# Queries and keys of attention: float16 parts split as rows and turned by DMA transposes, in place of identity products on TensorE

## The chip, the core and the metric

The program runs on one core of one Trainium2 chip. The core has these engines, each with its own queue of instructions that it works through in order: TensorE (PE, with its weight loads shown apart as PEld), VectorE (DVE), ScalarE (ACT), GpSimd (POOL) and SyncE (SP), which in this kernel issues nearly all DMAs. Sixteen DMA engines move the data. The metric is the device time of one execution in microseconds (us). One execution was also taken by the hardware profiler; its instructions, waits and transfers are the views that are shown here.

## The reference, cut to what matters

One layer of a transformer over 2048 rows (latents) and 256 rows (context) of width 1024: a modulated norm, one input projection, a retention branch and an attention branch, an output projection, and a feed-forward part. The change is in what attention does with its queries and keys, so only that is shown:

```python
q = _apply_rope(_rmsnorm(aq.reshape(B, L, ATT_HEADS, ATT_HD), q_norm_g), *att_cs)
k = _apply_rope(_rmsnorm(ak.reshape(B, L, ATT_KV_HEADS, ATT_HD), k_norm_g), *att_cs)
v = av.reshape(B, L, ATT_KV_HEADS, ATT_HD)
kc = _rmsnorm(cak.reshape(B, Lc, ATT_KV_HEADS, ATT_HD), k_norm_g)
...
k_all = jnp.concatenate([k_ctx, k_lat], axis=1)
...
s = jnp.einsum('bqkgd,bskd->bkgqs', q, k).astype(jnp.float32) * ATT_SCALE
p = jax.nn.softmax(s, axis=-1).astype(v.dtype)
return jnp.einsum('bkgqs,bskd->bqkgd', p, v)
```

There are 8 query heads and 2 key/value heads of width 64; four query heads share one key head. All inputs are float32.

## The kernel before, in words

*Accuracy by parts.* TensorE is given float16. A float32 operand is split into a high part, its rounding to float16, and a low part, the rest, also in float16. A score q.k is then q_hi k_hi + q_hi k_lo + q_lo k_hi. With a head width of 64 only half of TensorE's 128 rows are needed for one such product, so two of them are stacked in one matmul of 128 rows.

*First stage (0 to about 600 us).* The input projection. The rows come in 18 tiles of 128 (2 of context, 16 of latents) and in two groups: the first six tiles (context and latents 0 to 3), then latents 4 to 15. For each group and each block of columns of the weight (`C_RQ`, `C_RK`, `C_RV`, `C_RG` for retention, `C_AQ` for attention's queries, `C_AKV` for its keys and values) there is one *unit* per tile: 24 matmuls (8 blocks of depth, three products of parts) into one bank `pso`, of which there are five. The order of units is written out in `PLAN`: in the first group all `AKV` units follow each other, then all `AQ` units; in the second group `RK` and `AKV` alternate, then `AQ` and `RQ` alternate (from tile 15 down), then `RG`.

What happens to a unit's result is planned by hand. `post` hands pieces of work to `do(step, part, function)`: step s + 2 means "after the matmuls of the second unit from here". `run_step` emits a step's parts in the order of `PARTS`: hi, evac, turned, low, vec, pool, root, aux, turn, load, store. Since every engine works in order, this list is also the order of each queue. The steps carry much else: the weights' own splits, loads of later weights, the largest magnitudes of the feed-forward weights (`greatest_of`: a load one step, a DVE reduction `wmx` from `wm` the next), the forward states of retention.

*Queries (unit s of `AQ`).* ACT copies the bank to `xs` (L698), squares it (L658); DVE and POOL make norm and rotation (`rope`), the result is `ys` (L647, L649), 128 rows by 512 in float32. Step s + 4: four products with the identity turn it into `psx` in PSUM (L710, `turn`), so that rows become columns; partition 64 e + d then holds element d of head 2 j + e. Step s + 5: ACT makes the high part from `psx` (L781), DVE the low part (L784), both into `qhl`, a tile with tag `zs` (two buffers, shared with the turned retention queries and keys, L739). Step s + 6: the tile is stored to `aq` in DRAM (L788).

*Keys (unit s of `AKV`).* After norm and rotation `kn` holds keys as rows. Step s + 4: ACT makes the high part `kh` (L828). Step s + 5: DVE subtracts (L831), and `kn` holds key and low part beside each other. Step s + 6: two products with the identity (L836), one for each key head, give 128 partitions: 64 of the key and 64 of its low part. Step s + 7: DVE copies both into `ks` as float16 (L841), the tile from which all scores are made, 128 partitions by 2 heads by 2304 keys. At the end of the stage (L1521, L1522) `ks2` is made by DMA: the high parts again, in its lower 64 partitions, and a constant table `unit` in its upper 64.

*Second stage (about 600 to 1480 us).* Attention runs in 32 groups (16 query tiles, two key heads), 18 steps each, beside retention, the output projection and the start of the feed-forward part. `Group.load` fetches a group's queries `qr` 14 steps before its first use, with four DMAs of 64 KB: high parts in `qr[:, 0]`, low parts in `qr[:, 1]`, each in the lower and again in the upper 64 partitions. A first pass (`piece`, L177 and L181; `maximum`, L190) finds each query's largest score, with one matmul per 512 keys: `qr[:, 0]` against `ks`. Its shift is written as two float16 parts into the upper partitions of `qr[:, 1]` (`turn`, L204). The second pass (`scores`, L210 and L211) adds two matmuls, `ks` with `qr[:, 0]` and `ks2` with `qr[:, 1]`; `exp` follows, then the split of the weights and the product with the values. The first group's loads and first pass already run in the last units of the first stage.

*Third stage.* The feed-forward part, not touched.

Of the kernel before, what the change touches and what calls it, by code (L numbers as in the profile page):

```python
# [22 lines left out]
P = 128  # L23
# [9 lines left out]
HD = 64  # L33
# [23 lines left out]
def layer_kernel(ctx: ExitStack, tc: tile.TileContext, a: dict, out: bass.AP):  # L57
# [34 lines left out]
    aq_d = scratch("aq", NT, [P, 2, 4, P], F16)  # L92
# [56 lines left out]
    class Group:  # L149
# [7 lines left out]
        def load(self):  # L157
            pool, tag = (mq, "mb") if self.n % 4 < 2 else (qp, "qr")
            self.qr = pool.tile([P, 2, 4, P], F16, name="qr", tag=tag, bufs=2)
            q = self.qr.rearrange("p x (j e) t -> p x j e t", e=2)  # L160
            for e in range(2):
                src = aq_d[self.t][64 * e : 64 * e + 64, :, 2 * self.g : 2 * self.g + 2]
                nc.sync.dma_start(q[:64, :, :, e], src)
                nc.sync.dma_start(q[64:, :, :, e], src)
# [105 lines left out]
    with ExitStack() as st, tc.manual_schedule():  # L270
# [417 lines left out]
        def post(s, g, col, kind, i, x):  # L688
# [73 lines left out]
            elif col == C_AQ:  # L762
# [14 lines left out]
                do(s + 4, "turn", turn)  # L777

                def high():
                    x["z"] = op.tile([P, 2, 4, P], F16, name="qhl", tag="zs")  # L780
                    nc.scalar.activation(x["z"][:, 0], x["pt"], AF.Copy)  # L781

                def low():
                    nc.vector.tensor_tensor(x["z"][:, 1], x["pt"], x["z"][:, 0], op=ALU.subtract)  # L784

                do(s + 5, "turned", high)
                do(s + 5, "vec", low)
                do(s + 6, "store", lambda: nc.sync.dma_start(aq_d[i], x["z"]))  # L788
            else:
# [5 lines left out]
                def new_k():  # L795
                    x["kn"] = op.tile([P, 2, 2, HD], F32, name="kn", tag="kn", bufs=4)
                    return x["kn"][:, :, 0]

                r = lambda: bc(x["r"].unsqueeze(2), [P, 2, HD])
                if kind == "c":  # L800

                    def plain():
# [7 lines left out]
                        lambda: nc.vector.tensor_tensor(x["kn"][:, :, 0], x["kn"][:, :, 0], r(), op=ALU.mult),  # L810
# [15 lines left out]
                def high():  # L826
                    x["kh"] = op.tile([P, 2, HD], F16, name="kh", tag="kh")
                    nc.scalar.activation(x["kh"], x["kn"][:, :, 0], AF.Copy)  # L828

                def low():  # L830
                    nc.vector.tensor_tensor(x["kn"][:, :, 1], x["kn"][:, :, 0], x["kh"], op=ALU.subtract)  # L831

                def turn_k():
                    x["pt"] = psT.tile([P, 4, P], F32, name="psx", tag="psx")
                    for g in range(2):
                        nc.tensor.transpose(x["pt"][:, g], x["kn"][:, g].rearrange("p a b -> p (a b)"), ident)  # L836
# [3 lines left out]
                do(s + 6, "turn", turn_k)  # L840
# [1636 lines left out]
```

## Time and profile before

| | |
|---|---|
| median of 3 runs | 2655.08 us (2653.93 to 2656.46) |
| profiled execution, its own time | 2656.33 us |
| its span on the core | 2654.5 us |
| granted TensorE clock | 0.998 |
| first `L710` for queries to last query store | 122.5 to 564.2 us |
| DMA issued by SP, whole span | 478.94 MB, 54.8% of 16 engines |

The profile names lines of the kernel file (L710) and tiles by their names in the program. A row of a group has, in this order: engine, operation, output and inputs, shapes, count, busy time, mean duration of one, idle time of the engine just before and what ended it. A row of waits reads: engine and instruction, what it waited for, total us, times, longest. A row of one tile's instructions gives smallest, median and largest duration in ns, and the first and last start. "SPq" is a DMA issue on SyncE's queue; its duration is the time for which the issue holds that queue, and the time to landing is counted from the issue until the data have arrived. Matmuls overlap: a row of 0.38 us can start 0.22 us after the one before it.

### The profile page before, as it was taken

To read this page: it belongs to the slowest core of one execution; us is meant where nothing else is said; L and a number is where in the kernel's file an instruction comes from. 1 tells how busy PE (TensorE), PEld (TensorE's weight loads), DVE (VectorE), ACT (ScalarE), POOL (GpSimd) and SP (SyncE) were. 2 spreads that over 40 slices of the span, in tenths; PEclk is the share of its full clock that TensorE was granted. 3 is DMA by queue.
4 is the path that set the end of the run, shared out by engine and by line. 5 is a ranking of instruction groups with operands and counts; after the bars stand their busy time and mean duration, and the time that the engine had idled before them with its cause. 6 is when DMAs were issued, how large, how long until landed. Compare 5 with 4: busy or idle time off the path is not lost.

```text
span 2654.5 us, 45435 instructions
## 1 busy us (share of the span) xinstructions
PE 2601.0 (98%) x16617; PEld 1450.9 (55%) x16617; DVE 2049.4 (77%) x3099; ACT 1504.7 (57%) x2544; POOL 1761.7 (66%) x1451
## 2 busy tenths in 40 slices
PE   8999999998999999999999999999999999999998
PEld 5875555545666666666666444444444444444443
DVE  5778798677888888988987597889876656655686
ACT  3856343425877778788878575666665322222243
POOL 3644566545676668888887696677662666666686
PEclk9999999999999999999999999999999999999999
DMA  7876899746022123333422754776685757475453
GB/s 231 272 252 207 303 330 323 257 119 218 25 84 72 57 65 116 96 84 92 128 77 80 259 170 150 230 241 231 208 297 144 278 180 287 165 293 174 160 187 114
DMA packets 332903, 481.84 MB, mean 182 GB/s; under 512 B 90228, under 2 KB 200068, under 8 KB 328200
## 3 DMA queue, kind: packets, MB, share of 16 engines
q1 hardware_dynamic: 332664, 478.94, 54.8%
q8 instruction: 130, 2.13, 0.3%
q14 instruction: 93, 0.76, 0.1%
q10 hardware_dynamic: 16, 0.01, 0.0%
HBM read 321.89 MB, written 156.38 MB: 180 GB/s over the span
## 4 chain that ended last, share of the span: by engine, by line
PE 69%; ACT 3%; POOL 2%; DVE 1%; DMA 1%; issue 0%; SPq 0%; POOLq 0%; DVEq 0%; ACTq 0%
PE pd L2290 7%; PE pd L2289 7%; PE pd L2288 7%; PE pu L2063 7%; PE pu L2061 7%; PE pu L2062 7%; PE st L210 4%; PE o L245 4%; PE st L211 4%; PE mp L177 3%; PE o L243 2%; PE bank L1832 2%; PE bank L1830 2%; PE bank L1831 2%; ACT p L216 1%; ACT phi L220 1%
## 5 line engine op out<-in xcount | busy, mean ns | idle before, releaser
L190 DVE TENSOR_REDUCE nm<-mp 128x1 f32<-128x512 f32 x558 | 377.6, 685 | 90.7 <-PE mp L177 85.4
L216 ACT ACTIVATE p<-st 128x512 f32<-128x512 f32 x576 | 341.4, 600 | 162.7 <-PE st L211 156.3
L227 POOL TENSOR_TENSOR plo<-p,phi 128x1024 f16<-128x1024 f32 x160 | 348.2, 2181 | 87.1 <-ACT phi L220 87.0
L2063 PE MATMUL pu<-hf,w1f 128*128 128x512 f16 x896 | 339.6, 379 | 0.0
L2290 PE MATMUL pd<-w,uf 128*128 128x512 f16 x896 | 339.6, 379 | 0.0
L2061 PE MATMUL pu<-hf,w1f 128*128 128x512 f16 x896 | 339.6, 379 | 0.0
L2289 PE MATMUL pd<-w,uf 128*128 128x512 f16 x896 | 339.6, 379 | 0.0
L2062 PE MATMUL pu<-hf,w1f 128*128 128x512 f16 x896 | 339.6, 379 | 0.0
L2288 PE MATMUL pd<-w,uf 128*128 128x512 f16 x896 | 339.6, 379 | 0.0
L2308 POOL TENSOR_TENSOR y<-y,d 128x512 f32<-128x512 f32 x128 | 210.4, 1646 | 146.6 <-ACT uf L2277 99.9
L220 ACT ACTIVATE phi<-p 128x1024 f16<-128x1024 f32 x288 | 305.2, 1060 | 0.0
L229 DVE TENSOR_TENSOR plo<-p,phi 128x512 f16<-128x512 f32 x256 | 240.1, 939 | 21.8 <-ACT phi L220 9.4
L243 PE MATMUL o<-wv,plo 128*128 128x65 f16 x2304 | 230.7, 193 | 0.3 <-POOL plo L227 0.2
L245 PE MATMUL o<-wv,phi 128*128 128x129 f16 x2176 | 229.0, 220 | 0.0
L210 PE MATMUL st<-qr,ks 128*128 128x512 f16 x576 | 218.3, 379 | 8.6 <-ACT p L216 6.3
L243 PEld LDWEIGHTS <-plo 128*128 128x128 f16 x2304 | 205.5, 98 | 30.4 <-POOL plo L227 2.4
L2300 DVE SCALAR_TENSOR_TENSOR y<-pd,scy,y 128x512 f32<-128x512 f32 x160 | 116.9, 747 | 132.3 <-PE pd L2290 132.1
L211 PE MATMUL st<-qr,ks 128*128 128x512 f16 x576 | 218.5, 379 | 0.0
L2073 DVE TENSOR_TENSOR r<-pu,r 128x512 f32<-128x512 f32 x224 | 150.0, 684 | 82.8 <-PE pu L2063 58.3
L1191 PE MATMUL pso<-wf,h_l 128*128 128x512 f16 (+1 forms) x576 | 208.2, 361 | 0.0
L1192 PE MATMUL pso<-wf,h_l 128*128 128x512 f16 (+1 forms) x576 | 208.1, 361 | 0.0
L1193 PE MATMUL pso<-wf,h_l 128*128 128x512 f16 (+1 forms) x576 | 208.1, 361 | 0.0
(389 smaller groups left out, 6116.2 us busy)
## 6 DMA issues: line engine op xcount, KB each, us to landing
wm<-in_w_ff SPq DMA_DIRECT2D x64, 512.0 KB, 7.1
u<-r SPq DMA_DIRECT2D x128, 256.0 KB, 4.4
ur<-u SPq DMA_DIRECT2D x128, 256.0 KB, 5.9
y<-x SPq DMA_DIRECT2D x64, 512.0 KB, 6.5
wf<-w2f SPq DMA_DIRECT2D x112, 256.0 KB, 2.9
w<-wf SPq DMA_DIRECT2D x28, 1024.0 KB, 10.0
w1r<-in_w_ff SPq DMA_DIRECT2D x48, 512.0 KB, 5.3
x<-y SPq DMA_DIRECT2D x48, 512.0 KB, 2.6
```

What stands on the lines that cost most here:

```text
L190: nc.vector.tensor_reduce(dst, src, axis=AX.X, op=ALU.max, negate=True)
L216: nc.scalar.activation(self.p[kt // 2][:, kt % 2], self.s.pop(kt), AF.Exp, scale=HD**-0.5)
L220: nc.scalar.activation(hi, self.p[j], AF.Copy)
L227: nc.gpsimd.tensor_tensor(lo, p, hi, op=ALU.subtract)
L243: mm(o[:, : HD + 1], lo[:, i, c], v[:, : HD + 1], start=False, stop=False)
L245: mm(o, hi[:, i, c], v[:, :VW], start=False, stop=last)
L2061: mm(pu[hf, i], whi, hi, start=k == 0, stop=False)
L2062: mm(pu[hf, i], whi, lo, start=False, stop=False)
L2063: mm(pu[hf, i], wlo, hi, start=False, stop=k == 3)
L2288: mm(ps, u[:, 0, b], w[:, b, 0], start=b == 0, stop=False)
L2289: mm(ps, u[:, 0, b], w[:, b, 1], start=False, stop=False)
L2290: mm(ps, u[:, 1, b], w[:, b, 0], start=False, stop=b == 3)
```

## The change

The split is made before the turn. Queries stay rows: the tile `z` holds, for each head, 64 high and then 64 low parts, and it is stored so. Loading a group turns it: a DMA with `transpose=True` takes 128 rows by 512 columns (four heads of 128) and lays each head's 128 columns on 128 partitions. Each of the two halves of `qr` is loaded this way from the same rows, so both now hold high parts in the lower and low parts in the upper 64 partitions. For keys, ACT writes the high part twice side by side (`kk`), and a DMA transpose lays it straight into `ks`, high parts in both halves; the low parts (`kl`) are turned by a second DMA into `kt`, which is stored to DRAM two steps later; `ks2` reads its lower half from there. So `qr[:, 0]` with `ks` now gives q_hi k_hi + q_lo k_hi, and `qr[:, 1]` with `ks2` gives q_hi k_lo and the shift; before, the first gave q_hi k_hi + q_hi k_lo. The largest scores of the first pass are taken over the new sum.

```diff
-    aq_d = scratch("aq", NT, [P, 2, 4, P], F16)
+    aq_d = scratch("aq", NT, [P, 2, 4 * P], F16)
+    kl_d = dram.tile([P, NK, P], F16, name="kl", tag="kl")
...
         def load(self):
             pool, tag = (mq, "mb") if self.n % 4 < 2 else (qp, "qr")
             self.qr = pool.tile([P, 2, 4, P], F16, name="qr", tag=tag, bufs=2)
-            q = self.qr.rearrange("p x (j e) t -> p x j e t", e=2)
-            for e in range(2):
-                src = aq_d[self.t][64 * e : 64 * e + 64, :, 2 * self.g : 2 * self.g + 2]
-                nc.sync.dma_start(q[:64, :, :, e], src)
-                nc.sync.dma_start(q[64:, :, :, e], src)
+            for x in range(2):
+                nc.sync.dma_start(self.qr[:, x], aq_d[self.t][:, self.g], transpose=True)
...
-                do(s + 4, "turn", turn)
 
                 def high():
-                    x["z"] = op.tile([P, 2, 4, P], F16, name="qhl", tag="zs")
-                    nc.scalar.activation(x["z"][:, 0], x["pt"], AF.Copy)
+                    x["z"] = op.tile([P, 8, 2, HD], F16, name="qhl", tag="zs")
+                    nc.scalar.activation(x["z"][:, :, 0], heads(x["y"], 8), AF.Copy)
 
                 def low():
-                    nc.vector.tensor_tensor(x["z"][:, 1], x["pt"], x["z"][:, 0], op=ALU.subtract)
-
-                do(s + 5, "turned", high)
+                    nc.vector.tensor_tensor(x["z"][:, :, 1], heads(x["y"], 8), x["z"][:, :, 0], op=ALU.subtract)
+
+                def store():
+                    nc.sync.dma_start(aq_d[i].rearrange("p g n -> p (g n)"), x["z"].rearrange("p h a d -> p (h a d)"))
+
+                do(s + 4, "turned", high)
                 do(s + 5, "vec", low)
-                do(s + 6, "store", lambda: nc.sync.dma_start(aq_d[i], x["z"]))
+                do(s + 5, "store", store)
...
                 def high():
-                    x["kh"] = op.tile([P, 2, HD], F16, name="kh", tag="kh")
-                    nc.scalar.activation(x["kh"], x["kn"][:, :, 0], AF.Copy)
+                    x["kk"] = op.tile([P, 2, 2, HD], F16, name="kk", tag="kk")
+                    x["kl"] = op.tile([P, 2, HD], F16, name="kl", tag="kl")
+                    for e in range(2):
+                        nc.scalar.activation(x["kk"][:, :, e], x["kn"], AF.Copy)
 
                 def low():
-                    nc.vector.tensor_tensor(x["kn"][:, :, 1], x["kn"][:, :, 0], x["kh"], op=ALU.subtract)
+                    nc.vector.tensor_tensor(x["kl"], x["kn"], x["kk"][:, :, 0], op=ALU.subtract)
 
                 def turn_k():
-                    x["pt"] = psT.tile([P, 4, P], F32, name="psx", tag="psx")
-                    for g in range(2):
-                        nc.tensor.transpose(x["pt"][:, g], x["kn"][:, g].rearrange("p a b -> p (a b)"), ident)
+                    x["kt"] = op.tile([P, 1, P], F16, name="kt", tag="kt")
+                    to = ks[:, :, row * P : (row + 1) * P]
+                    nc.sync.dma_start(to, x["kk"].rearrange("p g e d -> p (g e d)"), transpose=True)
+                    nc.sync.dma_start(x["kt"], x["kl"].rearrange("p g d -> p (g d)"), transpose=True)
 
                 do(s + 4, "hi", high)
                 do(s + 5, "low", low)
-                do(s + 6, "turn", turn_k)
-                do(s + 7, "vec", lambda: nc.vector.tensor_copy(ks[:, :, row * P : (row + 1) * P], x["pt"][:, :2]))
+                do(s + 5, "store", turn_k)
+                do(s + 7, "store", lambda: nc.sync.dma_start(kl_d[:, row], x["kt"][:, 0]))
...
     ks2 = vp.tile([P, 2, NK * P], F16, name="ks2")
     for g in range(2):
-        nc.sync.dma_start(ks2[:64, g], ks[:64, g])
+        nc.sync.dma_start(ks2[:64, g], kl_d[64 * g : 64 * g + 64].rearrange("d n t -> d (n t)"))
         nc.sync.dma_start(ks2[64:, g], a["unit"])
```

The tiles `kk`, `kl` and `kt` come from the pool `op`, which gives two buffers to each tag.

More of the change, by code (lines that the diff above doesn't have):

```diff
@@ L795, in new_k @@
                 def new_k():
-                    x["kn"] = op.tile([P, 2, 2, HD], F32, name="kn", tag="kn", bufs=4)
-                    return x["kn"][:, :, 0]
+                    x["kn"] = op.tile([P, 2, HD], F32, name="kn", tag="kn", bufs=4)
+                    return x["kn"]
                 r = lambda: bc(x["r"].unsqueeze(2), [P, 2, HD])
```

2 lines of the change are left out of this document (1 added, 1 removed).

## The prediction

> **What bounds the kernel now.** I read the page first, then the busy time by stretches, then who waited for whom, then single instructions.
>
> ```profile
> span 2654.5 us, 45435 instructions
> PE 2601.0 (98%) x16617; PEld 1450.9 (55%) x16617; DVE 2049.4 (77%) x3099; ACT 1504.7 (57%) x2544; POOL 1761.7 (66%) x1451
> ...
> 300.00:425.00 125.00, 122.56 (x713) 70.26 (x712) 113.78 (x160) 53.65 (x97) 84.79 (x97) 1.00 0.95 339
> 425.00:600.00 175.00, 170.30 (x871) 87.84 (x869) 119.23 (x224) 56.22 (x91) 90.45 (x95) 1.00 0.64 207
> ...
> 660.00:2654.00 1994.00, 1973.34 (x13104) 1061.51 (x13101) 1552.33 (x2249) 1196.05 (x2005) 1414.62 (x1061) 1.00 0.48 158
> ```
>
> The columns of the stretches are window, length, busy time of PE, PEld, DVE, ACT and POOL, granted clock, DMA share, GB/s. PE is busy 98% of the span and of both stretches in which keys and queries are made (300 to 425 and 425 to 600 us); DMA is at 0.95 in the first. All of the edit's arithmetic lies before 660 us; the rest only follows. So the question is whether PE really sets the pace there. PE's waits between 0 and 660 us, longest first (total, times, longest):
>
> ```profile
> PE mp L177 <- DVE wmx L190: 3.6, 3, 2.1
> PE mp L177 <- ACT xs L698: 3.3, 2, 2.3
> PE mp L181 <- DVE wmx L190: 3.1, 1, 3.1
> ```
>
> The longest is 3.6 us: PE waits for almost nothing, so work taken from its queue there should shorten the stage, as long as no other queue takes over.
>
> **What is removed.** Four identity products per query tile (64 of the 192 of L710) and two per key tile (L836). Their durations overlap, so I take the price from start to start:
>
> ```profile
> 443.92 0.38 PE L1193 MATMUL pso<-wf,h_l 128*128 128x512 f16 x1
> 444.14 0.60 PE L710 MATMUL psx<-ident,ys 128*128 128x128 f32 x4
> 444.58 0.38 PE L1191 MATMUL pso<-wf,h_l 128*128 128x512 f16 x1
> ...
> 319.73 0.38 PE L836 MATMUL psx<-ident,kn 128*128 128x128 f32 x2
> 319.95 0.38 PE L1191 MATMUL pso<-wf,h_l 128*128 128x512 f16 x1
> ...
> L836 PE MATMUL psx<-ident,kn x36: 270/272/327, 99.5 to 417.9; 128*128 128x128 f32 x36
> L781 ACT ACTIVATE qhl<-psx x16: 587/597/598, 123.2 to 562.9; 128x512 f16<-128x512 f32 x16
> ```
>
> A set of four holds PE from 444.14 to 444.58 = 0.44 us, a pair from 319.73 to 319.95 = 0.22 us. With 16 query tiles (L781 x16) and 18 key tiles (36 / 2): 16 x 0.44 + 18 x 0.22 = 7.0 + 4.0 = **11.0 us**. More than this the edit can hardly give, since nothing later has less work: scores and maxima keep their products, only with the halves in other places.
>
> **What changes on VectorE and ScalarE.**
>
> ```profile
> L841 DVE CAST ks<-psx 128x256 f16<-128x256 f32 x18 | 7.5, 415 | 3.6 <-PE psx L836 3.6
> L784 DVE TENSOR_TENSOR qhl<-psx,qhl 128x512 f16<-128x512 f32 x16 | 11.0, 688 | 40.6 <-ACT qhl L781 40.6
> L494 DVE TENSOR_TENSOR h_l<-x_l,h_l 128x512 f16<-128x512 f32 x24 | 19.2, 842 | 0.0
> L828 ACT ACTIVATE kh<-kn x18: 293/309/312, 88.3 to 403.2; 128x128 f16<-128x128 f32 x18
> L831 DVE TENSOR_TENSOR kn<-kn,kh x18: 271/286/812, 98.1 to 413.4; 128x128 f32<-128x128 f32 x18
> ...
> 400.00:425.00 25.00, 24.40 (x122) 12.14 (x121) 24.58 (x35) 9.93 (x18) 18.72 (x18) 1.00 1.03 394
> ```
>
> DVE loses the copy into `ks` (18 x 0.415 = 7.5 us). Its query subtraction now has both sources in SBUF; the nearest row of that shape is L494, 842 against 688 ns: 16 x 0.15 = 2.5 us more. DVE gains 5 us, which matters only near 400 us, where it is busy 24.58 of 25: there the lighter DVE lets PE's gain pass. ACT makes the keys' high part twice, 18 x 0.309 = 5.6 us more, hidden, as it is busy 54 of 125 us. All this I cost at nothing; without its cover ACT's extra would cost at most those 5.6 us.
>
> One new wait: the keys' doubled high part has two buffers, and a buffer is free only when its transpose has landed. In the first group the first high part ran at 88.3 and the first subtraction only at 98.1 us, while key tiles follow each other closely. So ACT's third high part will stand behind a landing of some 5 us, with the evacuations and weight splits behind it, for which PE waits after its five banks. From 0 (the banks cover it) to about 5 us (one landing uncovered); I take 2, nearer to covered, since ACT can catch up during the wider query units that follow. In the second group key tiles are twice as far apart: nothing.
>
> The query path loses a step: high part at s+4 from SBUF, store one step earlier.
>
> ```profile
> ACT qhl L781 <- DMA aq<-qhl: 46.4, 11, 7.2
> DVE qhl L784 <- ACT qhl L781: 40.6, 10, 7.7
> ACT zs L739 <- DMA qt<-zs: 28.3, 9, 6.2
> ```
>
> Today ACT waits for an older query store to land before it may overwrite its buffer, and DVE waits behind ACT. Both tiles still share two buffers of tag `zs`; the high parts of queries and the retention copies now fall into the same step, so the two waits run together and DVE no longer follows directly. From a gain (the 3.3 us that PE lost behind ACT's evacuations come back) to an equal loss; I take 0.
>
> **What SP and the DMA engines get.** Per key tile two transposes and one store are added; per group four 64 KB loads become two transposes of 128 KB; the query store stays. No row shows a transpose. The nearest rows:
>
> ```profile
> L163 SPq DMA_DIRECT2D qr<-aq x64: 573/612/1095, 453.1 to 1381.6; - x64
> DMA to landing us min/median/max: 2.3/3.7/8.3
> L788 SPq DMA_DIRECT2D aq<-qhl x16: 320/382/913, 131.8 to 564.2; - x16
> L915 SPq DMA_DIRECT2D wm<-in_w_ff x32: 327/427/1026, 246.9 to 485.9; - x32
> ...
> q1 hardware_dynamic: 21610, 42.27, 95.0%
> wm<-in_w_ff SPq DMA_DIRECT2D x26, 512.0 KB, 6.4
> ...
> atb<-in_att_cs SPq DMA_DIRECT2D x12, 64.0 KB, 4.8
> ...
> mrow<-in_b_mod SPq DMA_DIRECT2D x2, 64.0 KB, 3.6
> ```
>
> The last four rows are DMA of 300 to 425 us: 13 rows, from `wm` x26 to `mrow` x2, 124 issues. At L915's 0.427 us, SP issues for 53 of 125 us, so it has 72 us for waits and new work. Twelve key tiles fall there. If a transpose holds SP like the costliest ordinary issue at hand (`qr`, 0.612 us), the addition is 12 x (2 x 0.612 + 0.382) = 19 us: it fits, and PE sees nothing. If it holds SP until its data land (3.7 us, the `qr` median), it is 12 x (2 x 3.7 + 0.382) = 93 us: 21 us too much. Bytes are no matter: 12 x 96 KB moved once and 32 KB more stored are 1.5 of 42.3 MB. I take the low end, because ordinary loads of like size leave SP after 0.6 us although they land after 3.7; the high end stays in the range as a rival. What queues behind a held SP are the loads for later steps, DVE's `wm` first.
>
> [...]
>
> In attention the issue time falls from 4 x 0.612 = 2.4 us a group to 1.2 (or rises to 7.4), in a group's 18 steps; loads are asked for 14 steps ahead, and DMA's share after 660 us is 0.48. Nothing. Two first uses are tighter:
>
> ```profile
> L177 PE MATMUL mp<-ks,qr x512: 376/379/514, 459.3 to 1430.9; 128*128 128x512 f16 x171
> L1521 SPq DMA_DIRECT2D ks<-ks x2: 532/657/782, 582.9 to 584.1; - x2
> L211 PE MATMUL st<-qr,ks x576: 377/379/634, 606.9 to 1461.2; 128*128 128x512 f16 x192
> ```
>
> The first `qr` load starts at 453.1 and is used at 459.3. Two transposes of 0.6 us that land after 3.7 are there at 458; if each takes twice that they come about 2 us late, once. I take 1. The low key parts, now read back from DRAM at 583, are needed at 607: nothing.
>
> **Sum.** 11.0 - 2 (first group) - 1 (first `qr`) = **8 us** less. The profiled execution took 2656.33 us (1.8 us around its span), so 2648.3; the median of the runs, 2655.08, lies 1.25 us lower, so 2647.
>
> **Rivals.**
>
> *Slower: a transpose holds SP's queue until it has landed.* Place: 300 to 425 us. For it: landings are long there (4.8 us for 64 KB) as DMA is at 0.95, and a transpose may hold its issuer, which no row excludes. Against: no ordinary issue in these rows does, at a median of 0.3 to 0.6 us. It decides from (72 - 12 x 0.382) / 24 = 2.8 us of hold per transpose, sooner if SP's own waits are counted. At 3.7 us the stretch grows by 21 us; against that stand the 8: 2647 + 21 = 2668. At 4.8 us it is 2647 + 47 = 2694. [...]
>
> *Given back: the time stays.* PE's gain on queries (7.0 us) goes because the steps there are paced by store landings (the 46.4 and 28.3 us of ACT waits); the 4.0 us of the keys less the 3 of losses remain: 2654. For it: those waits are per tile. Against: PE waited 3.3 us for ACT in the whole stage, so ACT's waits are covered today.
>
> *It isn't what it says: the turn is done element by element.* From the page's 54.8% of 16 engines over 332664 packets, a packet takes 0.07 us; 65536 two-byte packets on 16 engines would take 287 us a transpose, milliseconds in all. Nothing in the edit (runs of 128 elements on both sides) asks for it.
>
> ```profile
> q1 hardware_dynamic: 332664, 478.94, 54.8%
> ```
>
> **How the numbers follow.** Forecast 0.47, slower rival 0.33, given back 0.18, element by element 0.02. A measurement can't tell 0.2% (5.3 us) from no change. The forecast's own range is 2641 (all 11.0, and PE's 3.3 us behind ACT come back: 2655.1 - 14.3) to 2652 (five more of the uncertain losses); some of it lies within 0.2%, and part of the slower rival stays near zero when the hold is just over 2.8 us: faster 0.45, same 0.21, slower 0.34. The range 2641 to 2680 takes the rival at 3.7 us whole and leaves out its far end (about 0.12), the elements (0.02) and little below.
>
> **What would show it.** Right: sets of L710 at queries and L836 gone, and the stretch 300 to 600 us about 8 us shorter with PE still near 98%; the transposes' issue rows near 0.6 us on SP; DVE's wait for `wm` (3.0 us once today, below) not grown. Wrong: issue rows of 3 us and more, DVE waiting for `wm` in every step, PE gaps at `psx` or `pso` between 300 and 425 us; or ACT waiting for landings of `kk` near 100 us and PE with it; or as much PE gap between 430 and 600 us as products were removed.
>
> ```profile
> DVE wmx L918 <- DMA wm<-in_w_ff: 3.0, 1, 3.0
> ```

## The result, and the profile after

| | median | all runs | against before |
|---|---|---|---|
| before, beside it | 2655.43 us | 2653.93 to 2656.46 (4) | |
| after | 2675.30 us | 2671.63 to 2682.44 (4) | 1.0076 (95%: 1.0063 to 1.0088) |

The changed kernel is slower by 0.76%, some 20 us, where 8 us less were forecast. Its profiled execution took 2673.10 us, 2.2 less than the median, with a span of 2671.3 us, 16.8 more than before. The page's head, after:

```profile
span 2671.3 us, 45146 instructions
...
PE 2598.1 (97%) x16517; PEld 1444.9 (54%) x16517; DVE 2050.4 (77%) x3081; ACT 1509.7 (57%) x2562; POOL 1761.0 (66%) x1451
```

The 100 identity products are gone from PE, but its busy time fell only by 3 us. The busy time by stretches says where (the columns are those of the prediction):

```profile
125.00:150.00 25.00, 15.85 (x69) 12.46 (x67) 16.34 (x20) 10.78 (x20) 14.83 (x15) 0.91 0.70 231
150.00:175.00 25.00, 23.93 (x90) 17.85 (x91) 16.50 (x26) 16.99 (x29) 6.21 (x9) 0.82 0.70 256
...
375.00:400.00 25.00, 19.40 (x106) 11.69 (x104) 18.05 (x23) 9.07 (x15) 9.34 (x12) 0.86 0.82 269
...
300.00:425.00 125.00, 115.44 (x671) 67.48 (x669) 102.23 (x136) 52.08 (x101) 79.81 (x95) 0.96 0.91 286
425.00:600.00 175.00, 171.46 (x860) 86.72 (x859) 142.61 (x246) 64.37 (x107) 104.36 (x106) 1.00 0.82 263
```

Before, the first two of these stretches had PE busy at a clock of 1.00:

```profile
125.00:150.00 25.00, 25.00 (x120) 20.70 (x119) 21.16 (x30) 15.70 (x26) 13.99 (x12) 1.00 0.62 163
150.00:175.00 25.00, 23.35 (x107) 17.58 (x106) 19.69 (x40) 10.69 (x19) 8.75 (x12) 1.00 1.04 396
```

So PE loses 9 us in 125 to 150 us and 7 us in 300 to 425 us, and the matmuls that it does get done cost more, because the granted clock is below 1.00 there (0.91, 0.82 and 0.86 in the three rows of 25 us, 1.00 before in the first two). Who PE waited for from 0 to 660 us, after:

```profile
PE pso L1195 <- DVE wlo L538: 10.1, 5, 8.3
PE psx L708 <- DVE ys L645: 5.6, 1, 5.6
PE psx L708 <- ACT sq L656: 4.0, 1, 4.0
```

`wlo` is the low part of a retention weight, and L708 turns retention's rows: in all three rows PE waits to do retention's work, not a key's or a query's. What is late is what the other queues bring.

To put places and sizes together I matched products: the n-th matmul of the first product line (L1191 before, L1194 after, 776 of each in both) is the same work, and the difference of its start times is how far the changed kernel lags there. These are differences of starts in the PE timelines, in us; all kernels of the experiments stand in the same table, and the columns are the start before. Each row is one profiled execution; those of `held2`, `kt4` and `held4` took 4.3, 3.5 and 3.4 us more than their medians, that of `q_f16` 2.7 less, so differences of that size between rows say little.

```
start before      93.6  140.8  146.8  190.9  363.3  383.6  477.2  601.5
after             +0.6   -2.1  +12.7  +16.4  +14.9  +26.4  +26.6  +18.4
q_alone           +0.7   -1.2   -1.3   +1.2   +1.2   +1.3   -2.2  -10.4
k_alone           -0.1   +2.9   +8.2  +12.8  +11.3  +24.2  +30.5  +28.2
kt4               +0.5   -2.4   +1.1   +7.3   +5.8  +18.9  +18.4  +10.1
plain             +1.0   -1.9   +1.5   +7.3   +5.8  +10.6   +9.2   +1.5
plain_hold        -0.6   -4.1   -0.5   +4.8   +3.3  +14.6  +16.8   +8.5
k_one             +0.7   -0.7   +1.1   +8.4   +6.9  +11.3   +9.9   +7.1
k_one_kk4         +1.1   -0.3   -0.3   +1.6   +0.1   +4.4   +3.3    0.0
held2             +0.5   +0.3   +0.3   +1.9   +1.9   +0.8   +7.3   +6.5
held4             +1.0   +0.9   +0.9   +2.6   +2.6   +7.3  +15.1  +13.5
act4              -0.5   +8.6  +10.6  +17.8  +16.2  +24.8  +23.8  +15.6
q_full            +0.6   +5.9  +13.4  +15.9  +15.9  +17.6  +14.1   +5.8
q_f16             -0.7   -2.5   -0.7   +4.6   +4.2   +4.6   +0.9   -7.3
```

In the row "after": the gain runs as predicted up to 140.8 us, then 14.8 us are lost at one place in the first group and 3.7 right behind it, 11.5 more between 363 and 384 us, and behind 477 us the queries give 8 back. From 601 us to the end 1.6 us more come back. The two large losses have different causes in SP's queue.

**The first group.** SP's timeline, after (start, duration, queue, line, operation):

```profile
123.94 1.24 SPq L838 DMA_TRANSPOSE ks<-kk  x1
129.38 1.12 SPq L839 DMA_TRANSPOSE kt<-kl  x1
...
133.27 1.19 SPq L838 DMA_TRANSPOSE ks<-kk  x1
139.41 1.12 SPq L839 DMA_TRANSPOSE kt<-kl  x1
140.57 0.58 SPq L514 DMA_DIRECT2D wst<-in_w_in  x1
...
141.71 0.43 SPq L367 DMA_DIRECT2D wmo<-in_w_mod  x1
...
142.75 0.38 SPq L784 DMA_DIRECT2D aq<-qhl  x1
```

Between the first transpose of a tile and its second SP does nothing for 4 to 5 us. Its waits from 93 to 150 us name why:

```profile
SPq L839 <- DMA kl<-kt: 14.2, 4, 4.9
```

The second transpose writes `kt`, which has two buffers, and a buffer is free when the store `kl<-kt` (L844) of the tile two before has landed. That store itself was queued only two steps behind its own transpose. So SP stands, four times, and behind it stand the weights (`wst`, `wmo`) and the query store (`aq`), whose landing frees ACT's buffer:

```profile
148.08 0.63 ACT L778 ACTIVATE qhl<-ys 128x512 f16<-128x512 f32 x1 [11.77 <-DVE macc L378]
```

The profile puts ACT's 11.77 us down to `macc`; the store of 142.75 us has landed at 147.99 us by its semaphore, just ahead of the start at 148.08. ACT's weight split is behind it, DVE's `wlo` behind that, and then PE:

```profile
141.34 0.39 PE L1194 MATMUL pso<-whi,hhi_c 128*128 128x512 f32 x1
150.03 0.79 PE L1195 MATMUL pso<-wlo,hhi_c 128*128 128x512 f32 x1 [8.30 <-DVE wlo L538]
150.62 0.63 PE L1196 MATMUL pso<-whi,hlo_c 128*128 128x512 f32 x1
151.05 0.63 PE L1194 MATMUL pso<-whi,hhi_c 128*128 128x512 f32 x1
```

**Around 365 to 385 us.** There SP stands for no buffer of the new tiles; it is behind. The issue rows, after, with minimum, median and maximum in ns:

```profile
L838 SPq DMA_TRANSPOSE ks<-kk x18: 1192/1225/2212, 96.0 to 447.0; - x18
...
DMA to landing us min/median/max: 5.2/5.6/6.8
...
L839 SPq DMA_TRANSPOSE kt<-kl x18: 1119/1170/1271, 99.0 to 448.3; - x18
...
L162 SPq DMA_TRANSPOSE qr<-aq x64: 1188/1264/2373, 480.0 to 1398.3; - x64
...
DMA to landing us min/median/max: 2.6/3.3/6.9
```

The rows of landing follow only some transfers (3 of 18 of `ks`, 6 of 64 of `qr`); by the semaphores of all of them the medians are 5.2 us for `ks`, 3.3 for `kt` and 3.9 for `qr`. A transpose holds SP for 1.2 us, twice the 0.612 us that the prediction took, and the loads behind it come late. ACT's wait for the weights of the second group (`wf` from `wst`) in 345 to 385 us, before and after:

```profile
ACT wf L535 <- DMA wst<-in_w_in: 2.5, 1, 2.5
```

```profile
ACT wf L533 <- DMA wst<-in_w_in: 15.5, 4, 7.8
```

### The profile page after: what moved, and what is told of

Same layout as the page of the kernel before. It is cut to its first block, busy times and chain, and to the rows that moved or that the text cites. A ratio compares the mean times of both kernels' runs of the same rounds, so it can differ in the third digit from the quotient of the medians.

```text
span 2671.3 us, 45146 instructions
## 1 busy us (share of the span) xinstructions
PE 2598.1 (97%) x16517; PEld 1444.9 (54%) x16517; DVE 2050.4 (77%) x3081; ACT 1509.7 (57%) x2562; POOL 1761.0 (66%) x1451
## 4 chain that ended last, share of the span: by engine, by line
PE 80%; DMA 7%; ACT 5%; DVE 4%; POOL 2%; issue 1%; SPq 1%; ACTq 0%; DVEq 0%; POOLq 0%
PE pd L2293 7%; PE pd L2292 7%; PE pd L2291 7%; PE pu L2065 7%; PE pu L2066 7%; PE pu L2064 7%; PE st L208 4%; PE o L243 4%; PE st L209 4%; PE mp L175 3%; PE pso L1194 3%; PE pso L1196 3%; PE pso L1195 3%; PE o L241 2%; PE bank L1835 2%; PE bank L1833 2%
## 5 line engine op out<-in xcount | busy, mean ns | idle before, releaser
L1194 PE MATMUL pso<-wf,h_l 128*128 128x512 f16 (+1 forms) x576 | 209.6, 364 | 0.3 <-ACT sq L656 0.3
```

## The experiments

Theory 1: SP's in-order queue is the cause, by the hold of the transposes and by the wait for `kt`; what is lost is what the other loads and stores behind it are late. Theory 2: the transposes take the DMA engines' time. In each comparison "before" was run beside it on the same chip.

**The halves.** `q_alone` takes the key hunks back (keys by products, as before) and reads the low key parts from `ks[64:, g]`, so that a query's low part meets a key's low part and not its high part; `k_alone` takes the query hunks back. In it the low part goes into `kk` and a second high part into `kl`, so that every key transfer stays and the scores are whole:

```diff
 q_alone
-        nc.sync.dma_start(ks2[:64, g], kl_d[64 * g : 64 * g + 64].rearrange("d n t -> d (n t)"))
+        nc.sync.dma_start(ks2[:64, g], ks[64:, g])
 k_alone
-                    for e in range(2):
-                        nc.scalar.activation(x["kk"][:, :, e], x["kn"], AF.Copy)
+                    for to in (x["kk"][:, :, 0], x["kl"]):
+                        nc.scalar.activation(to, x["kn"], AF.Copy)
...
-                    nc.vector.tensor_tensor(x["kl"], x["kn"], x["kk"][:, :, 0], op=ALU.subtract)
+                    nc.vector.tensor_tensor(x["kk"][:, :, 1], x["kn"], x["kk"][:, :, 0], op=ALU.subtract)
```

> The queries' half of the change alone: keys are turned by products with the identity as before. The score of a query's low part with a key's high part is left out, with every instruction and transfer kept. Theory 1 (SP's in-order queue: the key tiles' transposes and the store of their low part hold it while the first stage needs it) and theory 2 (the transposes' own time on the DMA engines, which makes the other loads late) both put all the loss into the keys, because 64 query transposes fall into a stage in which the trace shows no loss: 16 sets x 0.44 us = 7 us less, 2646 to 2649 us. Theory 3 (the query loads also cost, which the key tiles' delay hides in the changed kernel): 2655 us or more.

> The keys' half of the change alone: the same two transposes, the same store and the same number of ScalarE and VectorE instructions for each key tile; the queries are turned by products with the identity as before. Theories 1 and 2: all of the loss and none of the queries' 7 us: the shift of 27 us that the changed kernel has at 475 us, less the idle time that vanished behind it, 2675 to 2682 us. Theory 3 (the halves cost alike): about 2665 us.

Measured: `q_alone` 2646.97 us, 0.9962 (0.9950 to 0.9975) of before; `k_alone` 2686.05 us, 1.0104 (1.0090 to 1.0118). The queries alone gain 10 us and all the loss is with the keys; theory 3 falls. `k_alone` is 4 us over its range: its lag reaches +30.5 us at 477 us, against +26.6 in the changed kernel, so the loss of the keys was somewhat larger without the queries than I worked out.

**The wait for `kt`.** Two more buffers, 256 bytes per partition each:

```diff
-                    x["kt"] = op.tile([P, 1, P], F16, name="kt", tag="kt")
+                    x["kt"] = op.tile([P, 1, P], F16, name="kt", tag="kt", bufs=4)
```

> The changed kernel with four buffers for the turned low part of the keys instead of two. Theory 1: the second transpose of a key tile no longer waits on SP for the store of the tile two before, so the 14.8 us at 141 to 147 us and most of the 3.5 us at 165 to 170 us go; the loss of some 12 us at 345 to 385 us stays: 2656 to 2661 us. Theory 2: the transposes run on the DMA engines as long as before, and little changes: 2673 to 2676 us.

Measured: 2662.75 us, 1.0018 (1.0009 to 1.0027): 12.6 us less than the changed kernel by the medians, 14.4 with each against its own before, 1.8 us over the range of theory 1, far from theory 2's. In the table the loss at 141 to 147 us shrinks from 14.8 to 3.5 us, and SP's wait for `kl<-kt` is no longer among its rows. The loss at 363 to 384 us stays (+13.1). What I had not expected is that 6 us are still lost from 147 to 191 us. Much of that can be the clock: the trace of `kt4` grants half of it from 169.4 to 176.2 and from 189.9 to 193.3 us, 10.2 us that are worth up to 5.1 us (an estimate: half the work at half the clock), and the kernel before has none between 93 and 640 us.

**One transpose for each key tile.** High and low part side by side in `kk`, as the products gave them; queries as before:

```diff
-                    for e in range(2):
-                        nc.scalar.activation(x["kk"][:, :, e], x["kn"], AF.Copy)
+                    nc.scalar.activation(x["kk"][:, :, 0], x["kn"], AF.Copy)
...
-                    nc.vector.tensor_tensor(x["kl"], x["kn"], x["kk"][:, :, 0], op=ALU.subtract)
+                    nc.vector.tensor_tensor(x["kk"][:, :, 1], x["kn"], x["kk"][:, :, 0], op=ALU.subtract)
...
-                    nc.sync.dma_start(x["kt"], x["kl"].rearrange("p g d -> p (g d)"), transpose=True)
...
-                do(s + 7, "store", lambda: nc.sync.dma_start(kl_d[:, row], x["kt"][:, 0]))
```

> Keys by one transpose for each tile (the high and the low part side by side, as the products with the identity gave them), no second transpose, no store of a turned low part; queries as before. Theory 1: one hold of 1.2 us on SP for each key tile and nothing that waits for a store: the products' 4 us come as a gain, and at most 4 us are lost to the hold: 2651 to 2655 us. Theory 2: two thirds of the turned bytes are left (32 of 48 KB a key tile) and so is two thirds of the loss of 25 us: about 2671 us.

Measured: 2662.17 us, 1.0017 (1.0008 to 1.0026), between the two theories and in neither range. The table shows why: the loss at 363 to 384 us is 4.4 us, as theory 1 has it, but 9 us are lost between 140.8 and 190.9 us, without any `kt`. ACT's waits from 93 to 125 us in this kernel:

```profile
ACT kk L829 <- DMA ks<-kk: 6.0, 2, 3.7
```

That is the buffer wait that the prediction put at 2 us. In the changed kernel it has nearly the same size:

```profile
ACT kk L830 <- DMA ks<-kk: 5.4, 2, 4.5
```

**That wait by itself.** The kernel with one transpose, with four buffers of `kk`:

```diff
-                    x["kk"] = op.tile([P, 2, 2, HD], F16, name="kk", tag="kk")
+                    x["kk"] = op.tile([P, 2, 2, HD], F16, name="kk", tag="kk", bufs=4)
```

> Keys by one transpose for each tile, queries by products, as before measured at 2662.2 us, with four buffers for the rows of key parts instead of two. Theory D (what is left of the first group's loss, 9 us, is ScalarE waiting 6.0 us for a key transpose's landing before it may write the next rows): ScalarE's wait goes and with it 4 to 8 us: 2654 to 2658 us. Theory E (the loss is SP standing at the transpose until VectorE has the low part, and the weights queued behind it; the buffers don't matter): 2660 to 2663 us.

Measured: 2657.32 us, 1.0009 (1.0000 to 1.0018), 4.9 us less than with two buffers by the medians, 3.2 with each against its own before: theory D, by its range. The lag at 190.9 us falls from +8.4 to +1.6. Some of that is the clock again: from 93 to 230 us `k_one` has 10.3 us at half of it, this kernel none. ACT's longest waits from 93 to 125 us are now

```profile
ACT zs L739 <- DMA kt<-zs: 2.6, 1, 2.6
ACT sq L658 <- DVE hs_q L663: 1.1, 1, 1.1
```

The changed kernel with more buffers of both `kk` and `kt` was not run.

**Hold or DMA engines.** From `kt4`, plain copies in place of the key transposes (`plain`), and then two small transfers added that only cost SP its time (`plain_hold`):

```diff
-                    nc.sync.dma_start(to, x["kk"].rearrange("p g e d -> p (g e d)"), transpose=True)
-                    nc.sync.dma_start(x["kt"], x["kl"].rearrange("p g d -> p (g d)"), transpose=True)
+                    nc.sync.dma_start(to, x["kk"].rearrange("p g e d -> p g (e d)"))
+                    nc.sync.dma_start(jk_d[row, 0:1], ident[:1])
+                    nc.sync.dma_start(x["kt"][:, 0], x["kl"].rearrange("p g d -> p (g d)"))
+                    nc.sync.dma_start(jk_d[row, 1:2], ident[:1])
```

(`plain` is this without the two `jk_d` lines.)

> The kernel with four buffers for the turned low part, but the two transposes of each key tile are plain copies of the same bytes between the same tiles: the keys are not turned, so the scores are others. Theory A (SP's queue is held 1.2 us by each transpose where a plain transfer holds it 0.6 us) and theory B (a transpose takes more of the DMA engines' time than its bytes do: in 325 to 425 us the kernel with one transpose for each key tile moved 328 GB/s for each full share of the engines, the kernel before 359) both say that the 12 us at 365 to 385 us go and the first group's loss shrinks: 2645 to 2652 us. Theory C (what costs is neither, but that the keys take two more transfers at all, or come late): 2660 us or more, as with four buffers and transposes.

> The same with plain copies, and behind each of the two copies one more transfer of 512 bytes on SP's queue, from a tile that never changes to a scratch row that nobody reads, so that SP is held as long as by the two transposes (2 x 0.6 us more for each key tile) while the DMA engines carry 1 KB more. Theory A: the loss comes back, 2659 to 2665 us. Theory B: no more than a microsecond over the kernel with plain copies, 2645 to 2653 us.

Measured: `plain` 2654.87 us, 0.9994 (0.9985 to 1.0003); `plain_hold` 2666.77 us, 1.0039 (1.0025 to 1.0053). Two transfers of 512 bytes for each key tile bring back 11.9 us, the loss at 363 to 384 us goes from 4.8 to 11.3 us, and nothing is transposed: theory A, 1.8 us over its range. How they add up on a full queue shows in SP's timeline of `plain_hold`:

```profile
374.87 0.61 SPq L839 DMA_DIRECT2D ks<-kk  x1
375.53 0.49 SPq L840 DMA_DIRECT2D jk<-ident  x1
376.06 0.49 SPq L841 DMA_DIRECT2D kt<-kl  x1
376.60 0.46 SPq L842 DMA_DIRECT2D jk<-ident  x1
377.10 0.34 SPq L733 DMA_DIRECT2D rk<-ys  x1
```

From 374.87 to 377.10 are 2.2 us, where the two transposes alone take 1.225 + 1.170 = 2.4. ACT's waits for `wst` in 345 to 385 us follow: in `plain`, `plain_hold` and `kt4` in turn

```profile
ACT wf L533 <- DMA wst<-in_w_in: 6.6, 2, 3.6
```

```profile
ACT wf L534 <- DMA wst<-in_w_in: 14.3, 4, 7.8
```

```profile
ACT wf L533 <- DMA wst<-in_w_in: 15.5, 4, 8.4
```

Theory B is not without ground: the same stretch in `kt4`, then in `plain`,

```profile
325.00:425.00 100.00, 89.34 (x497) 50.91 (x495) 81.16 (x106) 43.15 (x82) 54.01 (x67) 0.93 0.97 304
```

```profile
325.00:425.00 100.00, 94.09 (x540) 53.45 (x538) 87.31 (x112) 45.46 (x87) 62.11 (x74) 0.97 0.95 321
```

gives 304 / 0.97 = 313 GB/s for a full share of the DMA engines with transposes and 321 / 0.95 = 338 without. But `plain_hold`, without transposes, is no faster than `kt4`. Nor do the loads take longer once they are issued: between 308 and 413 us of the kernel before there are eight `wst` loads, which land after 6.3 us in the mean in that kernel, 6.4 in the change, 6.1 in `kt4`, 5.8 in `plain` and 5.4 in `plain_hold`. They are late because they are issued late. A small part for the DMA engines isn't excluded. `plain` is also 3 us above its range: plain copies too are three more transfers in a full queue, and the `kk` wait is still there.

**The queue of the kernel before, with nothing else changed.** Two (`held2`) and four (`held4`) small transfers for each key tile:

```diff
+                def held():
+                    for j in range(4):
+                        nc.sync.dma_start(jk_d[row, j : j + 1], ident[:1])
+
                 do(s + 5, "low", low)
+                do(s + 5, "store", held)
```

> The kernel before, and for each key tile two more transfers of 512 bytes on SP's queue, from a tile that never changes to a scratch row that nobody reads, queued in the step in which the changed kernel issues its transposes: 2 x 0.6 = 1.2 us of SP for each of 18 tiles, one transpose's hold, 18 KB in all for the DMA engines. By the prediction's account (72 us of SP free in 300 to 425 us, its entries early enough) nothing: 2653 to 2658 us. Theory 1 (SP's queue sets when the weights come): 3 to 6 us, the 5 us that the kernel with one transpose for each tile lost at 370 to 385 us: 2658 to 2662 us.

> The same with four such transfers for each key tile, 2.4 us of SP, two transposes' hold. By the prediction's account nothing: 2653 to 2658 us. Theory 1: 8 to 15 us, the 12 to 13 us that the changed kernel lost at 363 to 384 us and, in the first group, up to 3 us more: 2663 to 2671 us. If two cost much more than twice what one does, the queue has slack up to a point.

Measured: `held2` 2658.01 us, 1.0009 (1.0000 to 1.0018), at the border of both accounts; `held4` 2667.63 us, 1.0044 (1.0031 to 1.0057), inside theory 1's range. One assumption of both expectations was off: a transfer of 512 bytes holds SP less than 0.6 us. The row in `held4`:

```profile
L842 SPq DMA_DIRECT2D jk<-ident x72: 215/247/301, 96.2 to 431.2; - x72
```

So four of them hold SP for 1 us, less than one transpose. The place differs too: `held4` loses 5 us at 363 to 384 us and 8 more between 384 and 477 us. The queue has slack up to a point and none beyond it: the first two cost 1.9 us, the second two 9.6.

What four small transfers cost is then not mainly their hold. They depend on nothing but a constant, and yet SP waits at them, in `held4` from 300 to 425 us:

```profile
SPq L842 <- DMA wor<-in_w_out: 3.1, 3, 1.0
SPq L842 <- DMA wmo<-in_w_mod: 2.7, 3, 1.1
SPq L842 <- DMA wm<-in_w_ff: 2.5, 3, 1.1
```

In the traces the transfers report their landing on eight semaphores in turn, and nearly every issue waits for its own one, that is until the transfer eight entries before has landed: in the trace of the change 1422 of SP's 1436 issues name the semaphore of the issue eight before, and 1410 wait for it. So a new entry takes one of eight places as well as a hold. For the same 22 units, 308.2 to 412.6 us of the kernel before, SP's time divides like this (in us; the fourth column is waits for that landing, the fifth waits for an engine's result, the sixth, in `act4`, waits for other transfers):

```
             length   issue  between  eight back  engines  others
before        104.4    51.2      5.2        18.7     29.3     0.0
after         113.5    82.7      7.3        16.6      7.0     0.0
kt4           115.2    85.2      7.3        16.4      6.3     0.0
plain         106.8    69.1      6.2        25.0      6.5     0.0
plain_hold    113.3    72.2      7.9        26.7      6.5     0.0
held2         104.7    54.0      6.1        27.6     17.1     0.0
held4         109.7    55.2      6.6        35.7     12.2     0.0
act4          110.6    52.9      5.0        34.2      8.3    10.2
```

The room that the change took was in the waits for engines, 29 of 104 us before. It adds 31.5 us of issue, uses up 22 us of that room, and the stretch is 9 us longer. In `held4` the issues grow by 4 us and the waits for landings by 17, so it shows how little room the queue has, but not the price of a hold. For that, `plain` and `kt4` are the pair: 16 us more of issue, half of it made up by shorter waits for landings, 8 us more in all. In `plain_hold` the 6.5 us over `plain` are issue, landings and the time between entries together.

**Another queue.** `act4` is `kt4` with the two key transposes issued from ScalarE:

```diff
-                    nc.sync.dma_start(to, x["kk"].rearrange("p g e d -> p (g e d)"), transpose=True)
-                    nc.sync.dma_start(x["kt"], x["kl"].rearrange("p g d -> p (g d)"), transpose=True)
+                    nc.scalar.dma_start(to, x["kk"].rearrange("p g e d -> p (g e d)"), transpose=True)
+                    nc.scalar.dma_start(x["kt"], x["kl"].rearrange("p g d -> p (g d)"), transpose=True)
```

> The kernel with four buffers for the turned low part, and the two transposes of each key tile issued from ScalarE's queue instead of SP's. Theory A: SP is free of 2.4 us for each key tile, ScalarE (busy 10 of 25 us there) has room for them: the 12 us at 365 to 385 us go, 2648 to 2654 us. Theory B: the DMA engines do the same work and the 12 us stay, 2659 to 2666 us, or more where ScalarE's own work is held.

Measured: 2674.46 us, 1.0067 (1.0053 to 1.0080): slower than with SP, above both ranges. It doesn't tell the theories apart, since it moves the hold to a queue that is worse off, and the transposes take their places among the same eight semaphores from there: SP's waits for landings double (34 us against 16 in `kt4`). ACT's timeline in the first group:

```profile
114.20 1.21 ACTq L838 DMA_TRANSPOSE ks<-kk  x1
...
115.50 1.28 ACTq L839 DMA_TRANSPOSE kt<-kl  x1
116.83 1.06 ACT L529 ACTIVATE whi<-wst 128x1024 fp32r<-128x1024 f32 x1 [1.49 <-DVE t L632]
121.02 0.51 ACT L830 ACTIVATE kk<-kn 128x128 f16<-128x128 f32 x2 [3.12 <-DMA ks<-kk]
```

The hold of 1.2 us comes along, the `kk` wait stays (8.6 us from 93 to 125 us), and the lag is +8.6 us at 140.8 us. At 363 to 384 us `act4` loses 8.6 us against 13.1 in `kt4`.

**Versions that keep the queries' half.** `q_full` turns the key pair and the pair of low parts by two float32 products and lets ACT and DVE copy quarters of PSUM into `ks`; to make room it has two buffers of the tables `atb` instead of three:

```diff
-                x["tb"] = op.tile([P, 2, HD], F32, name="atb", tag="atb", bufs=3)
+                x["tb"] = op.tile([P, 2, HD], F32, name="atb", tag="atb", bufs=2)
...
+                        to, src = ks[64 * e : 64 * e + 64, g, c], x["pt"][64 * g : 64 * g + 64, 0]
+                        if eng:
+                            nc.vector.tensor_copy(to, src)
+                        else:
+                            nc.scalar.activation(to, src, AF.Copy)
```

> The queries turned by DMA transposes, the keys by two products with the identity for each tile as before, now the key pair itself and the pair of low parts; ScalarE and VectorE copy the quarters from PSUM to the score tiles, the turned low part is stored from a small tile, and nothing of the product is left out. Against the queries' half alone (2647.0 us) VectorE has about 0.2 us and ScalarE 0.5 us more for each key tile and SP one store of 0.6 us: both theories 2646 to 2651 us; more if VectorE, which is busy 24.6 of 25 us at 375 to 425 us, is the limit there: 2651 to 2654 us.

Measured: 2663.21 us, 1.0028 (1.0017 to 1.0039), a miss by 9 us. All of its loss is in the first group (+15.9 us at 190.9 us, almost nothing behind it). SP's longest wait from 93 to 150 us is for the buffer that I took away:

```profile
SPq L673 <- POOL att L677: 21.6, 3, 10.2
```

The same fault as the change's: a load that waits on SP for its own buffer, with everything else behind it. The copies on ACT may have a part in it; the run doesn't separate them.

`q_f16` keeps the changed kernel's split of the keys and turns it by three float16 products with a float16 identity, no buffer taken away:

```diff
+    ident16 = const.tile([P, P], F16, name="ident16")
+    nc.vector.tensor_copy(ident16, ident)
...
+                    for j in range(3):
+                        k = x["kl"] if j == 2 else x["kk"][:, j]
+                        mm(x["pt"][:, j], k.rearrange("p a d -> p (a d)"), ident16, start=True, stop=True)
+
+                def copy_k():
                     x["kt"] = op.tile([P, 1, P], F16, name="kt", tag="kt")
+                    nc.vector.tensor_copy(ks[:, :, row * P : (row + 1) * P], x["pt"][:, :2])
+                    nc.vector.tensor_copy(x["kt"][:, 0], x["pt"][:, 2])
```

> The queries turned by DMA transposes as in the changed kernel; the keys' float16 parts are split as there, but turned by three float16 products with a float16 identity for each tile, two VectorE copies from PSUM and the store of the turned low part; nothing of the product is left out. SP has one store more for each key tile than before and no transposes of keys, no buffer waits for a transpose's landing. Both theories as for the queries' half alone (2647.0 us), with up to 0.25 us more of ScalarE and 0.2 us more of VectorE for each key tile: 2645 to 2651 us. If ScalarE's second copy of the high part is what delays the first group by some 9 us in all kernels that have it: 2654 to 2658 us.

Measured: 2651.52 us, 0.9982 (0.9973 to 0.9991): faster than both kernels with the whole product kept, 4 us below before and 24 below the change. It falls half a microsecond above its first range; of the second, ScalarE's extra copy, some part may be true, as 5 us are lost between 147 and 191 us. Up to 3.4 of these are 6.8 us at half the clock; the run doesn't separate the rest.

## Why the prediction was wrong

**The sum failed at SP.** The step was "SP issues for 53 of 125 us, so it has 72 us for waits and new work ... it fits, and PE sees nothing". One number in it was off: a transpose holds SP 1.2 us, not 0.612. But with it the step would have come to the same answer, since 12 x (1.225 + 1.170 + 0.468) = 34 us (0.468 is the median of the store L844) still fit into 72. The account itself was wrong: not all of the time in which SP issued nothing was time that new entries could use. Of the 125 us SP issues for 60.7 in the kernel before, waits 20.6 for the landing eight entries back, spends 6.2 between entries and waits 37.5 for engines. That last part was the room, the 34 us use up nearly the whole of it, and the loads that stood behind came late (ACT's waits for `wst` in 345 to 385 us went from 2.5 to 15.5 us). `held4` shows it without the change: 1 us of issue for each key tile cost 11.5 us.

**It left out a stretch.** For SP the prediction counted 300 to 425 us only. In the first group the transposes cost an entry's own wait as well as its issue: 14.2 us of SP standing for `kt`, 12.6 us of the time (`kt4`). From 93 to 150 us SP waited 35.3 us for engines before and 3.8 after; by that sum the 14.5 us of added issue alone would have fitted, and the wait for `kt` is what did not. The prediction saw two buffers waiting for a landing at `kk` and not at `kt`, where the landing is a store's and the waiter is SP, with the weights of all engines behind it.

**A term of the right mechanism, too small.** ACT's wait for `kk`, "from 0 to about 5 us; I take 2": the wait is 5.4 us, and without it the kernel with one transpose gains 3 to 5 us. By that it was nearer the upper end, though in another kernel and with the clock in it.

**The slower rival.** It had the side, the queue and the victims (loads behind a held SP), but its mechanism doesn't hold: SP is held 1.2 us, while the data land after 5.2 us (`ks`) and 3.3 us (`kt`) in the median. By its own rule, slower from 2.8 us a transpose, the time should not have grown. The measured 2675.3 us lies inside the stated range of 2641 to 2680 only by the part that was added for this rival, and so by luck.

**What was right.** The products' price: in the changed kernel the lag falls by 0.2 us with each key tile and 0.4 us with each query tile, and `q_alone` has the queries' 7 us and 3 more. The first `qr` load: PE waits for it once, from 470 to 500 us,

```profile
PE mp L175 <- DMA qr<-aq: 1.0, 1, 1.0
```

the 1 us of the sum. Attention: the lag changes by no more than 1.6 us behind 601 us. The query path was costed at 0 between a gain of 3.3 us and a loss; it was the gain: PE's wait `mp <- ACT xs` of the profile before is not there in 480 to 560 us, and the queries alone give 10 us instead of 7. For the 7.5 us of `ks` copies no run shows an effect.

**The accounts together.** From the queries alone (2647.0) to the change (2675.3) are 28.3 us: the `kt` wait 12.6 (changed kernel to `kt4`), transposes in place of plain copies 7.9 (`kt4` to `plain`), and 7.9 for the copies' own transfers and the `kk` wait less the key products' 4 (`plain` to `q_alone`). The last is one number for several things; of them only the `kk` wait was measured alone, in another kernel. The runs come from several comparisons, whose medians of before differ by up to 2 us, so each of these terms is good to about that; with each kernel against its own before they are 14.4, 6.8 and 9.0 of 30.2 us. Part of every term is the clock: from 93 to 480 us the change has 27.3 us at half of it, `kt4` 23.8, `plain` 17.1, the kernel before none, and each such us costs up to half a us by the same estimate as for `kt4`.

## What to carry to other kernels

Before new entries go onto the queue that issues the loads, ask of each one what it waits for and what stands behind it; the busy share of the queue (60.7 of 125 us here) did not say it. Divide the queue's idle time by what ends it: here the room was in the waits for engines (37.5 of the 125 us; over the 22 units the change took them from 29.3 to 7.0) and hardly in the waits for landings (18.7 to 16.6). For an entry that writes a small buffer whose reader is a later entry of the same queue, count the buffers against the steps until that reader has landed (here two left SP standing for 14.2 us, and four in their place gave 12.6 us). And moving work from a busy engine to "free" transfers paid here for the queries (10 us), where two transposes took the place of four loads, 2.5 against 2.4 us of SP for each group, and not for the keys, where 2.9 us for each tile came on top of a queue whose loads arrive just in time.

## What the runs showed of the hardware

A DMA transpose of one to four blocks held SP's queue for 1.2 to 1.3 us in the median: 1.170 us for one block of 128 x 128 (`kt`), 1.225 for two (`ks`), 1.264 for four (`qr`); six on ScalarE's queue from 105 to 126 us in `act4` held that queue for 1.20 to 2.08 us, 1.26 in the median; a plain copy of the same bytes held SP 0.562 and 0.612 us (`kt` and `ks` in `plain`). The one block of `kt` landed after 3.3 us in the median, the two of `ks` after 5.2, the four of `qr` after 3.9. So the time to landing did not grow with the number of blocks, though these transfers differ in source and in load too. For the keys the products were the better turn, as what the transposes cost was mainly SP's queue (`q_f16`, with the keys' products, 2651.52 us against 2675.30 for the change); for the queries they were not (`q_alone`, with the queries' transposes, 2646.97 us, 0.9962 of before).

The gap of 8.30 us that ends at 150.03 us cost PE more than its length. Behind it the same kind of matmul starts every 0.43 us (150.62 to 151.05), against 0.23 ahead of it (141.11 to 141.34). Half the clock is granted from 145.37 to 159.02 us; the granted clock reads, after:

```profile
150.00:153.00 3.00, 2.50 (x5) 1.49 (x5) 0.00 (x0) 2.97 (x6) 0.00 (x0) 0.50 1.05 406
...
156.00:160.00 4.00, 4.00 (x15) 3.16 (x14) 1.63 (x7) 3.90 (x9) 1.75 (x2) 0.62 0.00 2
160.00:165.00 5.00, 5.00 (x23) 4.08 (x22) 4.93 (x7) 1.81 (x5) 2.21 (x3) 1.00 0.40 104
```

The lag of 14.8 us at that place is more than all of PE's waits for `wlo` in the stage (10.1 us); the rest is mostly the half clock. The way back to the full clock took 9.0 us from the end of the gap (150.03 to 159.02 us), the last 4.7 of them without another gap. Shorter gaps went with the half clock too, and not always: in the change PE stands 1.97 us until 180.77 and 1.62 us until 183.05, and half the clock is granted from 182.92 to 186.33 us; it stands 1.99 us until 200.18, and before 1.99 us until 183.76 at the same place of the program, and the clock stays at 1.00 both times.
